# The low part of q in the first block's attention scores: one zero-padded tile per head, so that both score products contract over 128 rows

## The chip, the cores and the metric

The kernel runs on one core of one Trainium2 chip. The metric is the device time of one execution in microseconds (us); less is better. The kernel before takes 2581.49 us (median of 3 runs, 2580.72 to 2582.58).

## The reference

Two transformer blocks of two layers each follow one another on x of 512 tokens by 1024 features. The change touches the two attention layers of the first block. Both have 16 heads of 64 features; the first is causal stick-breaking attention, the second mixes three dilated causal bands. Cut to the scores:

```python
# layer 0 of the first block
z = jnp.einsum('bhqd,bhkd->bhqk', qb, kh).astype(jnp.float32) * scale      # scale = 64 ** -0.5
log_stay = jnp.where(strict, jax.nn.log_sigmoid(-z), 0.0)
log_after = lax.cumsum(log_stay, axis=3, reverse=True) - log_stay
w = jnp.where(strict, jnp.exp(jax.nn.log_sigmoid(z) + log_after), 0.0)
out = jnp.einsum('bhqk,bhkd->bhqd', w, vh)
# layer 1 of the first block: q and k with rotary, three branches of (window, dilation)
z = jnp.einsum('brhnqd,brhnkd->brhnqk', qb, k_band).astype(jnp.float32) * scale
p = jnp.exp(z - max(z)); o = (p @ v) / sum(p)        # branches merged by their softmax denominators
```

The second block (a gated linear recurrence, a sliding-window attention, two convolutional MLPs) is not changed.

## The kernel before

All matrices are kept as sums of two rounded parts, high and low (`whi`/`wlo` of a weight block, `xh`/`xl` of the activations), and a product of two such sums is three TensorE products. Weights come through a ring of three staged blocks: SyncE loads a block (`wst`), in the second layer GpSimd multiplies it by a norm gain (L267), ScalarE makes `whi` (L286), VectorE makes `wlo` (L295).

The stages run one after the other: stick-breaking attention (`stick`), an MLP, dilated attention (`dilated`), an MLP, and then the second block, which holds the sliding-window attention (`window`). In each attention stage the heads are taken in eight pairs p = 0 to 7 of 128 features. `weave` writes two sequences alternately into the one program order of each engine: the large projections ("linear" work, pieces of some 24 products), and the attention steps. A step of `stick` makes the scores of one unit (`s1`: products over 128 rows, a mask product with `causal`, then `Abs`, `Exp`, `Ln` on ScalarE), the softplus and its two parts on VectorE (`s1b`), and the cumulative sums of the unit before (`s2`, products with `ntri` and `nones`). A step of `dilated` transposes the probabilities of the unit two steps back (`d2`, L1165, products with `ident`), makes the scores of a unit (`d1`), takes their maximum (L1144) and exponential, and normalizes the unit one step back (`dn`, L1157).

Within a head the 128 rows of TensorE are used like this. Tile `sk[h]` holds the high part of k in the head's own 64 rows and the low part in the other 64. Tile `sq[h]` holds the high part of q in the own rows and all of q in the others, so one product over 128 rows gives k_high·q_high + k_low·q. The missing k_high·q_low is a second product over the 64 own rows, with tile `ql`, which both heads of the pair share (head 0 has rows 0 to 63, head 1 rows 64 to 127). A unit's scores are therefore products of 128, 64, 128, 64 rows, one after the other, of 128, 256, 384 or 512 columns; such a group of four is called a quad below. There are 4 quads in a pair of heads, 32 in each of the two stages. In `stick` k is the operand that is loaded as weights, in `dilated` q is.

`pair_tiles` gives a pair its tiles: two rotating sets, and for every third pair (p = 2, 5) rows of the output tile `o` that are not yet written. `pair_k` (L487, L488) and `pair_q` (L495 to L497) fill them. The stage `window` of the second block already uses full-height second products: tiles `qp` (and two rows of `o`) whose unused half is set to zero once by GpSimd (L1487), with k and q packed in another way.

Of the kernel before, what the change touches and what calls it, by code (L numbers as in the profile page):

```python
# [8 lines left out]
F32 = mybir.dt.float32  # L9
F32R = mybir.dt.float32r  # L10
# [3 lines left out]
ALU = mybir.AluOpType  # L14
PSUM = bass.MemoryType.PSUM

P = 128
S = 512
# [182 lines left out]
class Ring:  # L201
# [3 lines left out]
    def next(self):  # L205
        self.i += 1
        return self.items[self.i % len(self.items)]


class Prog:  # L210
# [256 lines left out]
        run(side)  # L467


    def pair_tiles(self, pool, o, p):  # L470


        if p % 3 < 2:
            make = lambda n: pool.tile([P, S], F32R, name=n, bufs=2)
        else:
            room = iter([o[i][:, m, :] for m in (7, 6, 5) for i in (0, 1)])
            make = lambda n: next(room)
        t = {n: [make(f"{n}{h}") for h in (0, 1)] for n in ("sk", "sq")}
        t["ql"] = make("ql")
        return t  # L480

    def pair_k(self, t, src, eng=None):

# [7 lines left out]
    def pair_q(self, t, src, dup=None, eng=None):  # L491
        nc = self.nc
        for h in (0, 1):
            own, oth = slice(64 * h, 64 * h + 64), slice(64 - 64 * h, 128 - 64 * h)
            nc.scalar.activation(out=t["sq"][h][own], in_=src[own], func=AF.Copy)  # L495
            (dup or nc.vector).tensor_copy(out=t["sq"][h][oth], in_=src[own])
            self.defer(lambda h=h, own=own: (eng or nc.vector).tensor_tensor(  # L497
                out=t["ql"][own], in0=src[own], in1=t["sq"][h][own].bitcast(F32), op=ALU.subtract))

    def scores(self, out, t, h, lhs, ks, qs, start):  # L500

        own = slice(64 * h, 64 * h + 64)
        a = (t["sk"][h][:, ks], t["sq"][h][:, qs]), (t["sk"][h][own, ks], t["ql"][own, qs])
        for i, (k, q) in enumerate(a):
            self.mm(out, *((k, q) if lhs == "k" else (q, k)), start and i == 0)


# [352 lines left out]
    def stick(self):  # L860
        nc = self.nc
        lin, zr = Ring(self.bank[0:2] + self.bank[7:]), Ring(self.bank[2:6])
        with self.tc.tile_pool(name="stick", bufs=1) as pool:
            o = (pool.tile([P, KT, S], F32R, name="oh"), pool.tile([P, KT, S], F32R, name="ol"))
            identr, ntri = pool.tile([P, P], F32R, name="identr"), pool.tile([P, P], F32R, name="ntri")
            nones, causal = pool.tile([P, P], F32R, name="nones"), pool.tile([P, P], F32R, name="causal")
            consts = []
            for t, n in ((ntri, "ntri"), (causal, "causal")):
                e = pool.tile([P, S], F32, name="e", bufs=2)
# [2 lines left out]
            qk, vs = {}, {}  # L872

            def ev_q(s, c):
                def f(bank):
                    t = self.tmp.tile([P, S], F32, name="sq", bufs=3)
                    nc.vector.scalar_tensor_tensor(out=t, in0=bank, scalar=0.125, in1=self.r_bc, op0=ALU.mult, op1=ALU.mult)
                    qk[2 * s + c] = self.pair_tiles(pool, o, 2 * s + c)
                    self.pair_q(qk[2 * s + c], t)
                return f  # L880

# [171 lines left out]
    def dilated(self):  # L1053
        nc = self.nc
        lin, zr, tr = Ring(self.bank[0:2] + self.bank[7:]), Ring(self.bank[2:4]), Ring(self.bank[4:6])
        nc.scalar.preload_act_table_set("natural_log_exp_and_others")
        with self.tc.tile_pool(name="dil", bufs=1) as pool:
            o = (pool.tile([P, KT, S], F32R, name="oh"), pool.tile([P, KT, S], F32R, name="ol"))
# [2 lines left out]
            lnc = pool.tile([P, S], F32, name="lnc")  # L1061
            for t, n in ((cosr, "cos"), (sinr, "sin"), (lnc, "lncount")):
                self.load_const(t, n)
            qk, vs, st, due = {}, {}, {}, []

            def scaled():
# [12 lines left out]
            def ev_rope(p, part):  # L1079
                def f(bank):  # L1080
                    scale = 0.125 if part else 1.0
                    if not part:
                        qk[p] = self.pair_tiles(pool, o, p)
                    t2 = pool.tile([P, S], F32, name="t2", bufs=2)
                    t3 = pool.tile([P, S], F32, name="t3", bufs=2)
                    d = self.tmp.tile([P, S], F32, name="sq", bufs=3)
                    nc.vector.scalar_tensor_tensor(out=t2, in0=bank, scalar=scale, in1=sinr, op0=ALU.mult, op1=ALU.mult)
                    for a in range(0, P, 32):
                        dst, src = t3[a:a + 32, :], t2[a ^ 32:(a ^ 32) + 32, :]
                        if p:  # L1090
                            nc.sync.dma_start(out=dst, in_=src)
                        elif a < 64:
                            nc.scalar.activation(out=dst, in_=src, func=AF.Copy)
                        else:
                            nc.vector.tensor_copy(out=dst, in_=src)
                    nc.vector.scalar_tensor_tensor(out=d, in0=bank, scalar=scale, in1=cosr, op0=ALU.mult, op1=ALU.mult)
                    add = lambda: (nc.gpsimd if p else nc.vector).tensor_tensor(out=d, in0=d, in1=t3, op=ALU.add)
                    eng = nc.gpsimd if p > 1 else nc.vector
                    parts = lambda: self.pair_q(qk[p], d, eng, nc.gpsimd) if part else self.pair_k(qk[p], d, eng)
                    if p:  # L1100
                        due.append([7 if p == 1 else 3, add])
                        due.append([10 if p == 1 else 5, parts])
                    else:
                        add()
                        due.append([0, parts])
                return f
# [582 lines left out]
```

## Time and profile before

| | |
|---|---|
| median of 3 runs | 2581.49 us |
| the profiled execution | 2584.21 us, of it span 2582.3 us |
| TensorE (PE) busy | 2533.5 us, 98% of the span, 12732 products |
| VectorE (DVE), ScalarE (ACT), GpSimd (POOL) busy | 60%, 40%, 17% |
| stick-breaking attention with its projections | about 30 to 268 us of the span |
| dilated attention with its projections | about 660 to 906 us |
| sliding-window attention of the second block | from about 2037 us |

The busy time of PE is a sum of modelled durations of products that overlap; how fast products follow each other is read from their start times. A row of the timeline gives the start and the duration of an instruction (or, with xN, of several alike), its engine, its line, the tile written and the tiles read, and the shape: `64*128 64x256` is a product over 64 rows with 256 columns.

### The profile page before, as it was taken

What the parts mean: (1) busy time and instruction counts of PE and PEld (TensorE: products, weight loads), DVE (VectorE), ACT (ScalarE), POOL (GpSimd) and SP (SyncE); (2) the same over time, 40 slices, a digit from 0 to 9 for tenths busy, and PEclk for the clock granted to TensorE, in tenths of its full rate; (3) what the DMA queues carried; (4) which work ended last, traced back from release to release, by engine and by line L of the source; (5) the groups of instructions that cost most, each with busy time, mean ns of one, the idle gap of its engine ahead of it and who ended that gap; (6) DMA issues with size and microseconds to landing.
All of it is one profiled execution on the core that took longest, in us unless ns stands there. A gap on an engine that the chain in (4) does not pass through costs nothing.

```text
span 2582.3 us, 32942 instructions
## 1 busy us (share of the span) xinstructions
PE 2533.5 (98%) x12732; PEld 2097.1 (81%) x12732; DVE 1557.3 (60%) x2580; ACT 1045.8 (40%) x1736; POOL 443.6 (17%) x394
## 2 busy tenths in 40 slices
PE   9999999999999999999999999999999999999998
PEld 7777888888767788888888888788888777888887
DVE  7665643444767654444476667764556788745556
ACT  6666422223344442222333333443333574534243
POOL 2112100001545210000111124200102326100103
PEclk9999999999989999999999999899999999999998
DMA  4111222232312122222221112232322312232321
GB/s 146 51 49 48 92 98 98 89 102 96 103 58 77 62 96 92 98 98 99 98 95 58 66 37 78 82 113 92 98 97 83 107 50 74 93 103 88 100 93 55
DMA packets 71277, 220.19 MB, mean 85 GB/s; under 512 B 8741, under 2 KB 15013, under 8 KB 71120
## 3 DMA queue, kind: packets, MB, share of 16 engines
q1 hardware_dynamic: 70512, 216.57, 25.5%
q8 instruction: 100, 1.64, 0.3%
q0 software_dynamic: 464, 1.27, 0.2%
q14 instruction: 57, 0.47, 0.1%
q10 hardware_dynamic: 144, 0.25, 0.0%
HBM read 209.14 MB, written 5.24 MB: 83 GB/s over the span
## 4 chain that ended last, share of the span: by engine, by line
PE 88%; DVE 8%; ACT 2%; issue 1%; DMA 0%; SPq 0%; POOL 0%; DVEq 0%; ACTq 0%
PE bank L225 87%; DVE wlo L295 1%; DVE lt L640 1%; DVE pr L1548 1%; PE bank L1165 1%; ACT whi L286 1%; DVE pr L1157 0%; DVE pr L1535 0%; DVE ln_sm L545 0%; DVE hg L1265 0%; PE bank L1558 0%; DVE hq L1342 0%; DVE xl L653 0%; DMA x<-in_xT 0%; DVE sm L1538 0%
## 5 line engine op out<-in xcount | busy, mean ns | idle before, releaser
L286 ACT ACTIVATE whi<-wst 128x1024 fp32r<-128x1024 f32 (+2 forms) x410 | 411.1, 1008 | 936.5 <-PE bank L225 750.1
L225 PE MATMUL bank<-xh,whi 128*128 128x512 f32 (+1 forms) x1992 | 780.9, 392 | 7.3 <-DVE xh L650 4.8
L225 PE MATMUL bank<-xl,whi 128*128 128x512 f32 (+1 forms) x1992 | 773.5, 388 | 5.0 <-DVE xl L653 2.7
L225 PE MATMUL bank<-xh,wlo 128*128 128x512 f32 (+1 forms) x1992 | 770.5, 387 | 2.3 <-DVE wlo L295 2.3
L295 DVE TENSOR_TENSOR wlo<-wst,whi 128x1024 fp32r<-128x1024 f32 (+2 forms) x392 | 486.4, 1246 | 100.9 <-ACT whi L286 97.4
L225 PEld LDWEIGHTS bank<-xh,whi 128*128 128x128 f32 x1992 | 379.9, 191 | 90.3 <-issue 14.8
L225 PEld LDWEIGHTS bank<-xl,whi 128*128 128x128 f32 x1992 | 379.0, 190 | 85.8 <-DVE xl L653 6.8
L225 PEld LDWEIGHTS bank<-xh,wlo 128*128 128x128 f32 x1992 | 379.9, 191 | 74.4 <-DVE wlo L295 3.7
L225 PE MATMUL bank<-hh,whi 128*128 128x512 f32 (+1 forms) x760 | 285.4, 375 | 0.0
L225 PE MATMUL bank<-hl,whi 128*128 128x512 f32 (+1 forms) x760 | 284.2, 374 | 0.0
L225 PE MATMUL bank<-hh,wlo 128*128 128x512 f32 (+1 forms) x760 | 284.2, 374 | 0.0
L527 POOL TENSOR_TENSOR acc<-acc,sq 128x512 f32<-128x512 f32 x35 | 50.0, 1428 | 789.6 <-ACT sq L526 789.2
L770 DVE TENSOR_TENSOR x<-x,bank 128x512 f32<-128x512 f32 x96 | 65.9, 688 | 187.4 <-PE bank L225 187.4
L225 PEld LDWEIGHTS bank<-hh,wlo 128*128 128x128 f32 x760 | 143.2, 188 | 25.7 <-issue 0.5
L225 PEld LDWEIGHTS bank<-hh,whi 128*128 128x128 f32 x760 | 143.2, 188 | 25.7 <-issue 0.5
L225 PEld LDWEIGHTS bank<-hl,whi 128*128 128x128 f32 x760 | 143.2, 188 | 25.2
L574 POOL TENSOR_TENSOR x<-x,r_bc 128x512 f32<-128x512 f32 x32 | 46.5, 1462 | 480.4 <-ACT r_bc L572 419.9
L225 PE MATMUL bank<-whi,xh 128*128 128x256 f32 x416 | 122.0, 293 | 0.0
L225 PE MATMUL bank<-wlo,xh 128*128 128x256 f32 x416 | 119.5, 287 | 0.0
L225 PE MATMUL bank<-whi,xl 128*128 128x256 f32 x416 | 119.5, 287 | 0.0
L1410 DVE SCALAR_TENSOR_TENSOR b<-bank,vecs,b 128x511 f32<-128x511 f32 x88 | 65.9, 749 | 85.8 <-ACT b L1408 84.2
L1410 DVE SCALAR_TENSOR_TENSOR a<-bank,vecs,a 128x511 f32<-128x511 f32 x88 | 65.9, 749 | 83.8 <-ACT a L1408 82.2
(285 smaller groups left out, 3537.2 us busy)
## 6 DMA issues: line engine op xcount, KB each, us to landing
wst<-in_w SPq DMA_DIRECT2D x314, 512.0 KB, 3.2
wst<-in_w SPq DMA_DIRECT2D x64, 448.0 KB, 3.1
wst<-in_w SPq DMA_DIRECT2D x36, 256.0 KB, 2.7
t<-t SPq DMA_DIRECT2D x56, 64.0 KB, 2.0
rel_scratch<-sq SPq DMA_DIRECT2D x16, 192.0 KB, 2.1
x<-in_xT SPq DMA_DIRECT2D x8, 256.0 KB, 6.2
bias<-rel_scratch SPq DMA_DIRECT2D x16, 128.0 KB, 2.9
out_dram<-x SPq DMA_DIRECT2D x16, 128.0 KB, 1.8
```

The source lines that it names most:

```text
L225: self.nc.tensor.matmul(out, lhsT=l, rhs=r, start=start, stop=True, skip_group_check=True)
L286: self.nc.scalar.activation(out=self.split[i][0][:, 0:n], in_=self.staged[i][:, 0:n], func=AF.Copy)
L295: (eng or self.lo_eng or self.nc.vector).tensor_tensor(out=lo[:, 0:n], in0=st[:, 0:n], in1=hi[:, 0:n].bitcast(F32), op=ALU.subtract)
L527: self.defer(lambda: eng.tensor_tensor(out=self.acc, in0=self.acc, in1=sq, op=ALU.add))
L574: nc.gpsimd.tensor_tensor(out=self.x[:, j, :], in0=self.x[:, j, :], in1=self.r_bc, op=ALU.subtract)
L640: nc.vector.scalar_tensor_tensor(out=t, in0=self.x[:, m, cs], scalar=gm, in1=self.acc[:, cs], op0=ALU.mult, op1=ALU.mult)
L770: self.nc.vector.tensor_tensor(out=self.x[:, m, :], in0=self.x[:, m, :], in1=bank, op=ALU.add)
L1165: nc.tensor.transpose(bk[:, P * j:P * j + P], pr[h][:, P * j:P * j + P], self.ident)
L1410: nc.vector.scalar_tensor_tensor(out=t[:, sh:S], in0=bank[:, 0:S - sh], scalar=self.vec(f"cw{l}{tap}", f), in1=t[:, sh:S], op0=ALU.mult, o ...
L1548: nc.vector.tensor_scalar(out=pr[h][:, 0:W], in0=pr[h][:, 0:W], scalar1=sm[:, 4 + h:5 + h], scalar2=None, op0=ALU.mult)
```

## The change

`pair_tiles`, called once for each pair, is replaced by `pair_sets`, called once at the start of each of the two stages: three fixed sets, used by p % 3, each with a tile `ql` for each head. The half of `ql[h]` that isn't the head's own is set to zero there by GpSimd, six memsets of 64x512 in each stage. `pair_q` writes only the own half. `scores` multiplies all 128 rows of `sk[h]` with all 128 rows of `ql[h]`. Each set now has six tiles where it had five, two tiles more in SBUF for the two sets outside `o`, and the scratch space of the software DMA queue is cut to 4096 bytes per partition.

```diff
-    def pair_tiles(self, pool, o, p):
-        if p % 3 < 2:
-            make = lambda n: pool.tile([P, S], F32R, name=n, bufs=2)
-        else:
+    def pair_sets(self, pool, o):
+        sets = []
+        for n in range(3):
             room = iter([o[i][:, m, :] for m in (7, 6, 5) for i in (0, 1)])
-            make = lambda n: next(room)
-        t = {n: [make(f"{n}{h}") for h in (0, 1)] for n in ("sk", "sq")}
-        t["ql"] = make("ql")
-        return t
+            make = (lambda name: pool.tile([P, S], F32R, name=name)) if n < 2 else (lambda name: next(room))
+            sets.append({t: [make(f"{t}{h}_{n}") for h in (0, 1)] for t in ("sk", "sq", "ql")})
+            for h in (0, 1):
+                self.nc.gpsimd.memset(sets[n]["ql"][h][64 - 64 * h:128 - 64 * h].bitcast(F32), 0.0)
+        return sets
...
             self.defer(lambda h=h, own=own: (eng or nc.vector).tensor_tensor(
-                out=t["ql"][own], in0=src[own], in1=t["sq"][h][own].bitcast(F32), op=ALU.subtract))
+                out=t["ql"][h][own], in0=src[own], in1=t["sq"][h][own].bitcast(F32), op=ALU.subtract))
...
     def scores(self, out, t, h, lhs, ks, qs, start):
-        own = slice(64 * h, 64 * h + 64)
-        a = (t["sk"][h][:, ks], t["sq"][h][:, qs]), (t["sk"][h][own, ks], t["ql"][own, qs])
-        for i, (k, q) in enumerate(a):
+        k = t["sk"][h][:, ks]
+        for i, q in enumerate((t["sq"][h][:, qs], t["ql"][h][:, qs])):
             self.mm(out, *((k, q) if lhs == "k" else (q, k)), start and i == 0)
...
+            sets = self.pair_sets(pool, o)
...
-                    qk[2 * s + c] = self.pair_tiles(pool, o, 2 * s + c)
+                    qk[2 * s + c] = sets[(2 * s + c) % 3]
...
-    nc = bacc.Bacc("TRN2", target_bir_lowering=False, num_devices=1)
+    nc = bacc.Bacc("TRN2", target_bir_lowering=False, num_devices=1, dynamic_dma_scratch_size=4096)
```

On PE, VectorE, ScalarE and SyncE the sequence of instructions is the same before and after but for the names of tiles; on GpSimd twelve memsets come in, at two places. The first is the start of `stick`, between the sums of squares of the first norm (`acc`) and the loads of two constants (`e`, the masks `ntri` and `causal` before rounding); `sp` behind them belongs to the first attention step:

```order
-L527 TENSOR_TENSOR acc<-acc,sq 128x512 x7
+L526 TENSOR_TENSOR acc<-acc,sq 128x512 x7
+L479 MEMSET ql_0_203 64x512
+L479 MEMSET ql_0_204 64x512
+L479 MEMSET ql_1_211 64x512
+L479 MEMSET ql_1_212 64x512
+L479 MEMSET oh 64x512
+L479 MEMSET ol 64x512
 L238 DMA e<-in_consts 128x128 x2
 L950 TENSOR_TENSOR sp<-sp 128x128 x2
```

The two loads are now issued behind six memsets. The second place is the start of `dilated`, between the loads of the rotary tables and of the band table (`cosr`, `sinr`, `lnc`) and the gains of three staged weight blocks (`wst`):

```order
 L238 DMA cosr<-in_consts 128x512
 L238 DMA sinr<-in_consts 128x512
 L238 DMA lnc<-in_consts 128x512
+L479 MEMSET ql_0_4708 64x512
+L479 MEMSET ql_0_4709 64x512
+L479 MEMSET ql_1_4716 64x512
+L479 MEMSET ql_1_4717 64x512
+L479 MEMSET oh 64x512
+L479 MEMSET ol 64x512
 L267 TENSOR_TENSOR wst<-wst,vecs 128x1024 x3
```

Here the gains of three weight blocks stand behind the memsets.

## Rows read from the trace of the kernel before

**Rows 1.** The page: the chain that ended last, shares of the span by engine.

```profile
PE 88%; DVE 8%; ACT 2%; issue 1%; DMA 0%; SPq 0%; POOL 0%; DVEq 0%; ACTq 0%
```

**Rows 2.** Busy time by stretch: stick, start of dilated, rest of dilated; instructions in brackets.

```profile
41.00:262.00 221.00, 220.88 (x1180) 173.71 (x1179) 146.50 (x237) 151.96 (x298) 40.30 (x64) 1.00 0.16 53
686.00:752.00 66.00, 54.58 (x235) 39.19 (x234) 51.65 (x89) 25.38 (x58) 36.29 (x25) 0.87 0.27 80
752.00:904.00 152.00, 151.97 (x837) 117.62 (x838) 104.25 (x264) 73.70 (x177) 60.95 (x45) 1.00 0.22 67
```

**Rows 3.** Timeline of PE in stick: quads of 256, 128 and 512 columns.

```profile
41.16 0.28 PE L225 MATMUL bank<-sq,sk 128*128 128x256 f32 x1
41.37 0.38 PE L225 MATMUL bank<-ql,sk 64*128 64x256 f32 x1
41.68 0.39 PE L225 MATMUL bank<-sq,sk 128*128 128x256 f32 x1
...
42.31 0.33 PE L225 MATMUL bank<-sq,sk 128*128 128x128 f32 x1
...
43.33 0.50 PE L225 MATMUL bank<-causal,identr 128*128 128x256 f32 x2
...
57.74 0.39 PE L225 MATMUL bank<-sq,sk 128*128 128x512 f32 x1
...
59.34 0.44 PE L225 MATMUL bank<-causal,identr 128*128 128x128 f32 x2
```

**Rows 4.** Timeline of PE in window: quads whose four products all have 128 rows.

```profile
2055.42 0.28 PE L225 MATMUL bank<-sk,qp 128*128 128x128 f32 x1
...
2055.76 0.45 PE L225 MATMUL bank<-xh,whi 128*128 128x512 f32 x1
...
2057.20 0.28 PE L225 MATMUL bank<-sk,oh 128*128 128x256 f32 x1
...
2057.67 0.40 PE L225 MATMUL bank<-xh,whi 128*128 128x512 f32 x1
...
2061.06 0.36 PE L225 MATMUL bank<-sk,oh 128*128 128x256 f32 x1
2061.26 0.28 PE L225 MATMUL bank<-sk,qp 128*128 128x256 f32 x1
```

**Rows 5.** Timeline of PE in dilated: first row of and behind quads, 128 and 512 columns.

```profile
779.00 0.30 PE L225 MATMUL bank<-sk,sq 128*128 128x128 f32 x1
...
780.00 0.50 PE L225 MATMUL bank<-xh,whi 128*128 128x512 f32 x1
...
798.93 0.47 PE L225 MATMUL bank<-sk,sq 128*128 128x512 f32 x1
...
800.61 0.39 PE L225 MATMUL bank<-whi,xh 128*128 128x256 f32 x1
```

**Rows 6.** PE's waits, 660 to 906 us: us in total, times, longest.

```profile
PE bank L1165 <- DVE pr L1157: 8.2, 6, 3.6
```

**Rows 7.** Timeline of one dilated step: DVE's first and last work, PE's transposes behind it.

```profile
798.78 0.69 DVE L1087 SCALAR_TENSOR_TENSOR t<-bank,sinr 128x512 f32<-128x512 f32 x1 [1.73 <-PE bank L225]
...
803.85 0.75 DVE L1157 TENSOR_SCALAR pr<-pr,sm 128x384 f32<-128x384 f32 x2
...
805.02 0.82 PE L1165 MATMUL bank<-ident,pr 128*128 128x128 f32 x6
```

**Rows 8.** GpSimd's memsets of 64x512 in window, by tile: ns min/median/max.

```profile
L1487 POOL MEMSET qp<- x6: 518/519/662, 2007.3 to 2009.8; 64x512 f32 x6
```

**Rows 9.** Timeline at the two places of the memsets, and who uses what follows.

```profile
23.77 1.09 POOL L238 DMA_DIRECT2D e<-in_consts  x2
...
41.17 0.22 DVE L903 CAST ntri<-e 128x128 fp32r<-128x128 f32 x1
...
658.88 3.75 POOL L267 TENSOR_TENSOR wst<-wst,vecs 128x1024 f32<-128x1024 f32 x2
...
663.40 2.01 ACT L286 ACTIVATE whi<-wst 128x1024 fp32r<-128x1024 f32 x2 [6.80 <-PE bank L225]
```

More of the change, by code (lines that the diff above doesn't have):

```diff
@@ L1063, in dilated @@
                 self.load_const(t, n)
+            sets = self.pair_sets(pool, o)
             qk, vs, st, due = {}, {}, {}, []
@@ L1082, in f @@
                     if not part:
-                        qk[p] = self.pair_tiles(pool, o, p)
+                        qk[p] = sets[p % 3]
                     t2 = pool.tile([P, S], F32, name="t2", bufs=2)
```

## The prediction

> **What bounds the kernel now.** I read the page first: the chain that ended last is PE for 88% of the span [rows 1], so time that PE saves counts unless something takes its place. Next came the stretches of the two stages that change, since an average over the span says nothing of them [rows 2]. In the stick-breaking stage (41 to 262 us) PE is busy for 220.88 of 221 us, ScalarE for 152 and VectorE for 147: PE alone sets the pace. The dilated stage is two stretches. From 752 to 904 us PE is busy for 151.97 of 152 us, VectorE for 104. [...] Among PE's waits in this stage the longest in sum is that of the transposes for the normalized probabilities `pr`, 8.2 us in six waits, VectorE's work [rows 6]. Last I read single quads in the timeline, by start times.
>
> **What the change removes.** In stick a quad of 256 columns starts at 41.16 and the next at 42.31: 1.15 us for four products [rows 3]. Within it they start 0.31 us apart (41.37, 41.68), whether the step goes from 128 to 64 rows or back. The sliding-window stage makes the same sort of quad, two products into a bank, twice, with own weights for each, but all four over 128 rows: from 2057.20 to 2057.67, 0.12 us each [rows 4]. So a change of height costs some 0.19 us, and a stick quad has four: between its four products and in front of what follows. The clock isn't the reason: it is granted in full in this stretch [rows 2]. [...]
>
> Stick quads now: 128 columns 43.33 - 42.31 = 1.02 us; 256 columns 1.15; 512 columns 59.34 - 57.74 = 1.60; for 384 I take the mean of the last two, 1.38 [rows 3]. Sum 5.15 us for a head pair.
>
> The same quads at full height: 256 columns 0.47 [rows 4]. 128 columns: the last three products of such a quad take 2055.76 - 2055.42 = 0.34, 0.113 each, so 0.45 for four. 512 columns: between 2055.76 and 2057.20 lie six products of 512 columns, 0.24 each, so 0.96. 384 columns: the mean of 0.47 and 0.96, 0.71. Sum 2.59 us. A pair saves 5.15 - 2.59 = 2.56 us, eight pairs **20.5 us**.
>
> Dilated quads now: 1.00 us at 128 columns, 1.68 at 512 [rows 5]; the sizes in between by the mean 1.34, sum 5.36. At full height the first product behind transposes starts its successor after 0.20 us (2061.06 to 2061.26) and not 0.12 [rows 4], so each quad costs 0.08 more than in stick; and the quad that is followed by products with 64 output columns keeps a switch of another kind, for which I take 0.1, an estimate between nothing and the 0.19 of a change of height. Sum 2.59 + 0.32 + 0.10 = 3.01. A pair saves 2.35 us; the six pairs from 752 us on **14.1 us**, the two before it 4.7.
>
> **What of it is lost.** In stick no other engine comes near: with 20 us gone ScalarE is busy for 152 of some 201 us. I take off 1 us for steps at the stage's end where exponentials hand a bank back late, an estimate; bounds 0 and 3. In dilated the margins are narrow. VectorE works without a break from 798.78 to 804.60, from the end of a column of linear work on PE to the last `pr`, and the transposes that need it start at 805.02: 0.42 us of room [rows 7]. The quad between them loses 1.68 - 1.04 = 0.64, so PE then waits 0.2, and 0.3 where the room is less. I allow 0.3 for one step in four of the 24 in this stretch: 1.8 us, bounds 0 and 7 (every step). In the 66 us before, where VectorE sets the pace, what PE saves mostly turns into longer waits for `pr`; the bounds are 0 and 4.7, and I take 2, as PE's quads do stand in the chain in places. [...]
>
> **What the change adds.** Rows of zeros cost PE nothing beyond the full-height pace: the window quads read above have them too, in `qp`. Six memsets of 64x512 are put on GpSimd's queue in each stage; at 0.52 us [rows 8] that is 3.1 us twice. In stick they delay the loads of the mask constants from 23.77 to 26.9; VectorE takes them at 41.17, 14 us later [rows 9], and GpSimd's next work is an attention step's: nothing. In dilated they stand in front of weight gains: two gains take 658.88 to 662.63, so 1.87 each, and would now run from 662.0 to 665.7. ScalarE begins two `whi` at 663.40; the first has its gain from earlier, the second (at about 664.4) needs the first of these two, done at 663.9: 0.5 us of room. If that cover were gone, ScalarE, then `wlo`, then the norm's statistics behind `wlo` on VectorE would be late by the same amount, at worst 1 us. I take 0. The smaller descriptor scratch changes no instruction; I take 0, with 0 and 5 us as bounds (an early load of three that had to wait for another's landing). VectorE's and ScalarE's work is the same in number and size.
>
> **Sum.** 20.5 - 1.0 + 14.1 - 1.8 + 2.0 = 33.8 us. The profiled execution took 2584.21 us, so 2550.4 for one like it; that run lies 2.7 us above the median, and the prediction goes by the median: 2581.49 - 33.8 = **2548 us**, 1.3% less.
>
> **Rivals.**
> - *VectorE takes over in dilated.* If its chain from projection to `pr` is as tight in all steps as at 798.78, PE's saving in this stage turns into waits: 20.5 - 1 = 19.5, so 2562 us. For it: 0.42 us of room [rows 7]. Against it: VectorE has 48 us idle of 152, and one wait per step costs at most 0.3 of 0.6 saved. Chance 0.13.
> - *All of it and the clock.* No step is bound elsewhere and the half-clock stretch goes: 20.5 + 14.1 + 4.7 + 8.6 = 47.9, so 2534 us. For it: denser products. Against it: VectorE's waits remain. Chance 0.08.
> - *The change doesn't do what it says.* The 0.19 us comes from something else in these quads (two products in a row into one bank, new weights each time) and stays: 2581 us, with 1 us for memsets 2582. Against it: the window stage's quads have both and run at 0.12. Chance 0.03.
> - *Slower by the clock.* [...] Chance 0.02.
> - *Slower by lost overlap.* If the half-height products of head 0 (rows 0 to 63) and head 1 (rows 64 to 127) ran beside other products, 64 of the 128 would be free today, and at full height cost 0.12 to 0.24, 0.18 on average: 11.5 us, 2593. [...] It decides where a half-height product now takes less of PE's time than a full one; it takes 0.31 against 0.12 [rows 3, 4], as a full-height product always stands between two of them. Chance 0.01.
>
> **How the numbers follow.** The forecast's own case has 0.73 and spans 2542 to 2554 (loss terms at their bounds in part). To leave out no more than 2 in 10, the range reaches towards the first two rivals: **2539 to 2560 us**. A change within 0.2% (5 us, about what this kernel's measurement can tell from none) comes from the third rival, 0.03; slower by more from the last two, 0.03; faster has 0.94.
>
> **What would show it.** In the changed profile products of `ql` read 128*128, a 256-column quad in stick takes about 0.5 us, and the stretch from the first to the last quad in stick is some 20 us shorter. In dilated from its first full PE stretch on it is 12 to 14 us shorter, with waits of PE for `pr` of a few tenths. Wrong would be: starts still 0.3 us apart; more half clock than 17 us in dilated; `whi` in ScalarE waiting for a gain near 664 us; waits for `pr` in every step.

## The result and the profile after

The changed kernel took **2542.16 us**, the median of 4 runs (2539.21 to 2547.36), beside 2581.1 us before (4 runs, 2579.26 to 2582.58): a ratio of **0.9852, 95% interval 0.9833 to 0.9871**. The forecast was 2548 us in a range of 2539 to 2560. The profiled execution took 2539.21 us, with a span of 2537.4; beside the profiled one of before (2584.21) that is 45.0 us less, so some 6 us of what the two traces show is more than the medians do. Where these 6 us lie matters below.

The page of after, busy time by engine and the shares of the chain that ended last:

```profile
PE 2485.7 (98%) x12732; PEld 2085.5 (82%) x12732; DVE 1558.2 (61%) x2580; ACT 1044.8 (41%) x1736; POOL 452.1 (18%) x406
PE 87%; DVE 8%; ACT 2%; issue 1%; DMA 1%; SPq 0%; POOL 0%; DVEq 0%; ACTq 0%; POOLq 0%
```

PE still is 87% of the chain [rows 1], with the same 12732 products in the same order; the 12 more instructions on GpSimd are the memsets. The stick quads of after, as [rows 3] shows those of before:

```profile
40.79 0.28 PE L225 MATMUL bank<-sq,sk 128*128 128x256 f32 x1
40.91 0.28 PE L225 MATMUL bank<-ql,sk 128*128 128x256 f32 x1
41.03 0.28 PE L225 MATMUL bank<-sq,sk 128*128 128x256 f32 x1
41.15 0.28 PE L225 MATMUL bank<-ql,sk 128*128 128x256 f32 x1
41.27 0.22 PE L225 MATMUL bank<-sq,sk 128*128 128x128 f32 x1
...
55.27 0.39 PE L225 MATMUL bank<-sq,sk 128*128 128x512 f32 x1
55.49 0.39 PE L225 MATMUL bank<-ql,sk 128*128 128x512 f32 x1
...
56.17 0.33 PE L225 MATMUL bank<-causal,identr 128*128 128x128 f32 x2
56.34 0.39 PE L225 MATMUL bank<-sph,ntri 128*128 128x384 f32 x1
```

Products of `ql` now have 128 rows and start 0.12 us behind the one ahead, not 0.31; a quad of 256 columns takes 0.48 us where it took 1.15, one of 512 columns 0.90 where it took 1.60. The stretches that answer to [rows 2], each from the first quad of its stage to just behind the last, with dilated split at the third pair's first quad (length, then PE, PE's loads, DVE, ACT, POOL busy, granted clock, DMA share, GB/s):

```profile
40.79:232.34 191.55, 191.40 (x1149) 164.87 (x1147) 141.93 (x230) 146.22 (x286) 40.44 (x62) 1.00 0.18 59
663.60:721.39 57.79, 45.26 (x238) 35.64 (x237) 49.12 (x89) 25.44 (x58) 36.87 (x25) 0.94 0.30 92
721.39:852.18 130.79, 128.86 (x801) 107.24 (x800) 101.23 (x251) 68.86 (x170) 61.68 (x45) 1.00 0.22 69
```

Between the same instructions of before lie 214.72, 66.32 and 144.24 us, so the stages gave 23.2, 8.5 and 13.4 us, and nothing else in the kernel moved by more than 1.2: from the stick stage to the first dilated quad it takes 431.27 us instead of 430.07, behind dilated 1685.2 instead of 1685.8, and ahead of stick 40.79 instead of 41.16. The six differences add to 44.9, the difference of the two spans. In dilated PE is no longer busy without a break: 1.9 us of 130.79 are idle, where before there was none. Its waits for the normalized probabilities in that stretch (us in sum, times, longest), of after:

```profile
PE bank L1166 <- DVE pr L1158: 1.2, 2, 1.0
PE bank L1166 <- ACT pr L1150: 0.7, 1, 0.7
```

### The profile page after: what moved, and what is told of

Read it like the earlier page. It is cut to its first block, busy times and chain, and to the rows that moved or that the text cites. A ratio compares the mean times of both kernels' runs of the same rounds, so it can differ in the third digit from the quotient of the medians.

```text
span 2537.4 us, 32954 instructions
## 1 busy us (share of the span) xinstructions
PE 2485.7 (98%) x12732; PEld 2085.5 (82%) x12732; DVE 1558.2 (61%) x2580; ACT 1044.8 (41%) x1736; POOL 452.1 (18%) x406
## 4 chain that ended last, share of the span: by engine, by line
PE 87%; DVE 8%; ACT 2%; issue 1%; DMA 1%; SPq 0%; POOL 0%; DVEq 0%; ACTq 0%; POOLq 0%
PE bank L225 86%; DVE wlo L295 1%; DVE lt L639 1%; DVE pr L1549 1%; PE bank L1166 1%; ACT whi L286 1%; DVE pr L1536 0%; DVE ln_sm L544 0%; DVE pr L1158 0%; DVE hg L1266 0%; PE bank L1559 0%; DVE hq L1343 0%; DVE sm L1539 0%; DVE xl L652 0%; DVE pr L1145 0%
## 5 line engine op out<-in xcount | busy, mean ns | idle before, releaser
L225 PEld LDWEIGHTS bank<-xh,whi 128*128 128x128 f32 x1992 | 378.9, 190 | 86.7 <-issue 13.5
```

The costliest lines, as they stand in the source:

```text
L225: self.nc.tensor.matmul(out, lhsT=l, rhs=r, start=start, stop=True, skip_group_check=True)
```

## The experiments

Profiles of one kernel differ by several microseconds in the stretch in which dilated starts, so whole times come from several runs, and the stages from each kernel's own trace. All ratios are to the kernel before on the same chip: 2583.09 us (17 runs) for the first four, 2582.71 us (15 runs) for the next four; the last three are single runs for their profiles.

**Each stage alone.** `e1_stick_only` keeps the old tiles and heights in dilated, `e2_dilated_only` keeps them in stick; the stage that keeps them has no memsets either. Against the changed kernel, the first (the second has the same in the stick stage):

```diff
     def scores(self, out, t, h, lhs, ks, qs, start):
-        k = t["sk"][h][:, ks]
-        for i, q in enumerate((t["sq"][h][:, qs], t["ql"][h][:, qs])):
+        own = slice(64 * h, 64 * h + 64) if "half" in t else slice(0, P)
+        a = (t["sk"][h][:, ks], t["sq"][h][:, qs]), (t["sk"][h][own, ks], t["ql"][h][own, qs])
+        for i, (k, q) in enumerate(a):
...
-                        qk[p] = sets[p % 3]
+                        qk[p] = self.pair_tiles(pool, o, p)
```

> Full-height second products in the stick-breaking stage alone; the dilated stage as before. If each change between 64 and 128 rows costs PE some 0.19 us and nothing else matters, this stage gives the 23 us that the two traces show between its first and last quad (quads 41.2 us before, 20.1 after, and 0.05 us less on each product behind a quad): 2581 - 23 = 2558 us, and the half-clock stretches of the dilated stage stay at about 17 us. If a part of the gain comes from the sets or the scratch and not from the height, it is another number.

> Full-height second products in the dilated stage alone. If the two stages add up, it gives the rest of the 39 us: 2581 - 16 = 2565 us. If the lesser half clock in the dilated stage (17 us of it before, 7 in the profile of the changed kernel) belongs to the change, the profile has about 7 us of it again and the time may be as low as 2560; if it is chance, it may have 17 and the time is up to 2570.

Measured: 2556.16 us (4 runs, 2552.19 to 2557.91), ratio 0.9899 (0.9884 to 0.9913), and 2567.88 us (6 runs, 2566.11 to 2571.52), ratio 0.9948 (0.9936 to 0.9959). The shares, 1.01% and 0.52%, add to 1.53%; both together gave 1.48%. The windows of the first, in the order of those above:

```profile
40.66:232.18 191.52, 191.38 (x1148) 164.94 (x1147) 141.87 (x230) 146.14 (x286) 40.45 (x62) 1.00 0.18 59
662.24:721.47 59.23, 53.13 (x239) 39.87 (x237) 48.38 (x89) 25.65 (x58) 36.24 (x25) 0.88 0.30 89
721.47:865.71 144.24, 144.21 (x802) 111.10 (x800) 99.49 (x253) 69.84 (x170) 60.66 (x45) 1.00 0.21 63
```

and of the second:

```profile
41.02:255.75 214.73, 214.60 (x1149) 168.26 (x1147) 142.69 (x230) 146.15 (x286) 39.44 (x62) 1.00 0.16 52
687.21:751.25 64.04, 47.68 (x238) 37.74 (x237) 52.70 (x89) 25.67 (x58) 36.76 (x25) 0.89 0.27 83
751.25:884.06 132.81, 129.28 (x801) 107.22 (x800) 103.09 (x251) 68.86 (x170) 61.31 (x45) 1.00 0.23 68
```

The first and third line of each show a stage that depends on its own quads alone: 191.5 us with full height and 214.7 without, 132.8 with and 144.2 without. The middle line goes against the quads: it is short (59.2) where dilated is unchanged and long (64.0) where it is changed. What shortens this stretch is something else.

**All but the height.** `e3_all_but_height` is the changed kernel, with its sets, memsets and smaller scratch, but the second product of a score again takes its head's 64 rows alone:

```diff
-        k = t["sk"][h][:, ks]
-        for i, q in enumerate((t["sq"][h][:, qs], t["ql"][h][:, qs])):
+        own = slice(64 * h, 64 * h + 64)
+        a = (t["sk"][h][:, ks], t["sq"][h][:, qs]), (t["sk"][h][own, ks], t["ql"][h][own, qs])
+        for i, (k, q) in enumerate(a):
```

> All of the change (fixed sets, a ql tile for each head, twelve memsets, the smaller scratch), but the second product again over the head's own 64 rows. If the height alone makes the gain, the time is that of the kernel before and the memsets' price, 2581 to 2583 us, with quads as long as before (1.15 us at 256 columns). If the sets or the placement in memory make part of it, it lies under 2575.

Measured: 2583.09 us (12 runs, 2577.02 to 2585.38), ratio 0.9999 (0.999 to 1.0009). Its PE timeline is that of before [rows 3], 0.3 us apart:

```profile
41.02 0.28 PE L225 MATMUL bank<-sq,sk 128*128 128x256 f32 x1
41.23 0.38 PE L225 MATMUL bank<-ql,sk 64*128 64x256 f32 x1
41.53 0.39 PE L225 MATMUL bank<-sq,sk 128*128 128x256 f32 x1
...
42.16 0.33 PE L225 MATMUL bank<-sq,sk 128*128 128x128 f32 x1
```

So the whole gain is the height of the second product; the tiles, the memsets and the scratch together give and cost nothing that the whole time can tell.

**The half-height products side by side.** `e4_halves_together` is the kernel before with the order within a quad changed: both heads' first products, then both heads' second products. Each quad then has two changes of height in place of four, and the two half-height products, on rows 0 to 63 and 64 to 127 and into different banks, are neighbours:

```diff
-                    for h in (0, 1):
-                        self.scores(banks[h][:, o0:o0 + S - P * j], qk[p], h, "k", slice(P * j, P * j + P), slice(P * j, S), n == 0)
+                    for part, h in ((0, 0), (0, 1), (1, 0), (1, 1)):
+                        self.scores(banks[h][:, o0:o0 + S - P * j], qk[p], h, "k", slice(P * j, P * j + P), slice(P * j, S), n == 0, part)
...
-                for h in (0, 1):
-                    self.scores(banks[h][:, 0:W], qk[p], h, "q", slice(0, W), slice(P * i, P * i + P), True)
+                for part, h in ((0, 0), (0, 1), (1, 0), (1, 1)):
+                    self.scores(banks[h][:, 0:W], qk[p], h, "q", slice(0, W), slice(P * i, P * i + P), True, part)
```

> The kernel before, with the four products of a quad in another order: the two of 128 rows, then the two of 64 rows (the same work, the same tiles). If the cost is one of changing the height, a quad has two changes where it had four, a 256-column quad takes about 1.15 - 0.38 = 0.77 us, and the 64 quads give up to 24 us, less the dilated stage's waits: about 2561 us. If it is a cost of each half-height product, whatever stands beside it, quads stay at 1.15 us and the time at 2581. If half-height products on different rows also run beside each other, the two start a few ns apart and a 256-column quad takes about 0.65 us: 2556.

Measured: 2554.3 us (4 runs, 2551.72 to 2556.51), ratio 0.9893 (0.9879 to 0.9908). Its PE timeline, a stick quad of 512 columns (the view puts products alike into one row; x2 is two):

```profile
56.01 0.62 PE L225 MATMUL bank<-sq,sk 128*128 128x512 f32 x2
56.55 0.50 PE L225 MATMUL bank<-ql,sk 64*128 64x512 f32 x2
56.98 0.44 PE L225 MATMUL bank<-causal,identr 128*128 128x128 f32 x2
```

The two products of `ql` stand in one row of 0.50 us, where a single one of them has 0.497 us in the kernel before (the mean of twelve), so by an estimate from these two figures they start some 8 ns apart at most; and the two together pass in the 0.43 us that a single one took before. Even so the quad takes 0.97 us where full height takes 0.90: one product of 0.23 us is hidden, but the two changes of height cost more than that, 0.97 - 3 x 0.227 = 0.29 us (0.227 us is the mean of three steps at full height, 55.27 to 55.95 in after). Stick takes 198.55 us in this order, 214.72 before and 191.55 after.

**The memsets.** `a1_changed_again` is the changed kernel once more, `e5_memsets_on_vector` has the dilated stage's six memsets on VectorE:

```diff
-                self.nc.gpsimd.memset(sets[n]["ql"][h][64 - 64 * h:128 - 64 * h].bitcast(F32), 0.0)
+                eng.memset(sets[n]["ql"][h][64 - 64 * h:128 - 64 * h].bitcast(F32), 0.0)
...
-            sets = self.pair_sets(pool, o)
+            sets = self.pair_sets(pool, o, nc.vector)
```

> The changed kernel once more, unchanged, for a second profile. If the lesser half clock at the start of the dilated stage (7 us against 17) belongs to the changed kernel, it is there again and the two profiles agree in that stretch within 1 us. If it is chance of the execution, the half clock lies anywhere from 7 to 17 us and the stretch differs by up to 5 us, while the stick stage and the rest of the dilated stage agree within 0.3 us.

> The changed kernel with the six memsets of the dilated stage on VectorE, which is idle there for 8 us, and not on GpSimd. If the memsets push the weight gains on GpSimd so that these run beside wlo on VectorE and slow it (two wlo took 3.67 us, 2.36 before), PE's wait for dg falls from 1.3 us to some 0.6 and the first quad of the dilated stage comes 1.2 us earlier against the last of stick; the whole time is 1 us less, within the spread of runs. If the memsets cost nothing, nothing moves.

Measured: 2541.94 us (4 runs, 2538.88 to 2545.65), ratio 0.9841 (0.9825 to 0.9856), and 2542.44 us (5 runs, 2538.59 to 2545.49), ratio 0.9842 (0.9827 to 0.9856): not to be told apart by the whole time, where 1 us less was expected of the second. By the stage they are: from stick to the first dilated quad the memsets on VectorE give 429.96 us, those on GpSimd 431.3, the kernel before 430.1. The timeline of after, at the place of [rows 9]:

```profile
635.23 2.19 POOL L479 MEMSET ql<- 64x512 f32 x4
637.46 0.52 POOL L479 MEMSET oh<- 64x512 f32 x1
638.04 0.52 POOL L479 MEMSET ol<- 64x512 f32 x1
638.53 3.73 POOL L267 TENSOR_TENSOR wst<-wst,vecs 128x1024 f32<-128x1024 f32 x2
639.73 2.01 ACT L286 ACTIVATE whi<-wst 128x1024 fp32r<-128x1024 f32 x2 [6.80 <-PE bank L225]
640.83 3.67 DVE L295 TENSOR_TENSOR wlo<-wst,whi 128x1024 fp32r<-128x1024 f32 x2 [8.37 <-ACT whi L286]
644.41 0.15 DVE L552 TENSOR_SCALAR small<-bank 128x4 f32<-128x4 f32 x1
```

and of the kernel with the memsets on VectorE:

```profile
632.37 2.37 DVE L479 MEMSET ql<- 64x512 f32 x4 [0.17 <-issue]
...
640.57 2.36 DVE L295 TENSOR_TENSOR wlo<-wst,whi 128x1024 fp32r<-128x1024 f32 x2 [4.57 <-ACT whi L286]
642.85 0.15 DVE L552 TENSOR_SCALAR small<-bank 128x4 f32<-128x4 f32 x1
```

ScalarE's `whi` doesn't wait: 2.01 us for the two, as before. But GpSimd's gains, 3.3 us later than they would be, now run from 638.53 to 642.26, and the second of them beside the first of VectorE's two `wlo`: this one takes 2.53 us instead of 1.23, the other 1.21 as ever, so the two take 3.67 us instead of 2.36. The norm's statistics behind them are 1.3 us late, and PE waits for what is made of them (tile `dg`) for 1.6 us instead of 0.6. The second gain and the first `wlo` of after by themselves, and the same `wlo` with the memsets on VectorE:

```profile
640.38 1.88 POOL L267 TENSOR_TENSOR wst<-wst,vecs 128x1024 f32<-128x1024 f32 x1
640.83 2.53 DVE L295 TENSOR_TENSOR wlo<-wst,whi 128x1024 fp32r<-128x1024 f32 x1 [8.37 <-ACT whi L286]
...
640.57 1.23 DVE L295 TENSOR_TENSOR wlo<-wst,whi 128x1024 fp32r<-128x1024 f32 x1 [4.57 <-ACT whi L286]
```

If `wlo` stands still until the second gain ends, the two end at 642.26 + 2.36 = 644.62; they end at 644.50, and in `e3`, which has the same memsets, the same sum gives 668.17 where 668.03 is measured. So in both traces the first `wlo` is late as if it stood still until the gain ends, to 0.14 us; what holds it isn't shown.

**The clock where dilated starts.** What the middle stretch shows is part chance. One more profile of after and two more of before were taken for it:

> The kernel before, unchanged, profiled again. If where the half clock falls at the start of the dilated stage is chance, the 66 us from that stage's first quad to the second quad of p = 2 take another time here, by 2 to 8 us, with the same instructions; if the first profile is typical, 66 us within 1 us and half clock of about 17 us.

> As the run before it: a third profile of the kernel before, for the same stretch; chance gives three values spread over several us, a typical first profile three equal ones.

> A third profile of the changed kernel. The stretch took 57.8 us in the first and 60.5 in the second; if the change itself shortens it by 2 us and the rest is chance, the three lie about 2 us under the three of the kernel before on average, with overlapping spreads; if it shortens it by 6 us or more, all three lie under all three of before.

Measured: 2576.36 and 2583.14 us before, 2545.86 after (one run each). Windows of that stretch, from the first dilated quad to the third pair's: of the kernel before,

```profile
685.95:752.27 66.32, 54.90 (x239) 39.51 (x237) 51.70 (x89) 25.65 (x58) 36.61 (x25) 0.87 0.27 80
```

of its second profile,

```profile
686.13:745.58 59.45, 52.71 (x239) 39.10 (x237) 48.53 (x89) 25.37 (x58) 36.54 (x25) 0.89 0.29 89
```

and of its third,

```profile
687.12:751.09 63.97, 54.59 (x239) 39.57 (x237) 50.12 (x89) 25.64 (x58) 36.62 (x25) 0.87 0.27 83
```

then of `a1_changed_again`,

```profile
663.43:723.93 60.50, 46.96 (x238) 37.90 (x237) 51.29 (x89) 25.43 (x58) 36.93 (x25) 0.92 0.29 88
```

and of `a2_changed_third`:

```profile
663.65:728.11 64.46, 47.62 (x239) 37.14 (x237) 53.06 (x89) 25.55 (x58) 36.80 (x25) 0.89 0.27 82
```

Before: 66.3, 59.5, 64.0, mean 63.2. After: 57.8, 60.5, 64.5, mean 60.9. The granted clock is 0.87 to 0.94 in the mean. In the two profiles first compared it is either 1.00 or 0.50 in this stretch, and 0.50 in pieces: before from 690.6 to 694.0, 711.1 to 721.3 and 738.4 to 741.8 us, after from 679.5 to 682.9 and 706.8 to 710.2. At 0.50, half clock, the means stand for 7 to 17 us (0.87 over 66.32 us is 2 x 0.13 x 66.32 = 17): in the order of the profiles 17, 14 and 17 us before, 7, 10 and 14 after. Within either kernel the shortest stretch is the one with the least half clock; across the two this doesn't hold, since 14 us go with 59.5 before and with 64.5 after. The kernel's own gain of 2.3 us in the means is smaller than the spread of either kernel; three profiles each don't settle it. What all three show is a turn of work into waits: PE is busy for 54.1 us of the stretch in the mean before and for 46.6 after, and idle for 9.2 and 14.3.

The rest of dilated wasn't as steady as `a1_changed_again` expected: behind this stretch the changed kernel takes 130.8, 132.8 and 130.7 us in its three profiles, not the same within 0.3; before it was 144.2 each time.

To see what the half clock costs, `e6_fill_before` is the kernel before with ten more products in front of the second and the fourth step of dilated, into a bank that nobody reads, and `e7_fill_after` the same in `e5_memsets_on_vector`. They add work and take none away:

```diff
+                    for _ in range(10 if t in (1, 3) else 0):
+                        self.mm(self.bank[6], self.xn[0][:, 0, 0:P], self.xn[0][:, 0, :], True)
```

> The kernel before with 20 more products of 512 columns, whose result nobody reads (10 each ahead of two steps at the start of the dilated stage, in an idle bank, where PE waits for VectorE). They cost 4.6 us of PE at full clock. If the half-clock stretches there (17 us in the profile) cost what they seem to (up to 8.6 us) and come from PE's waits, they shrink and the time falls to 2575-2580 us or stays; if VectorE alone sets the pace there and the clock costs nothing, the time is that of before or up to 4.6 us more.

> The changed kernel with the memsets of the dilated stage on VectorE and the same 20 unread products. If the clock is what spreads its runs (2539 to 2547 us), half clock in that stretch is gone, the runs lie closer together and at 2537 to 2541 us; if not, the time is 2542 us or up to 4.6 us more.

Measured: 2578.6 us (11 runs, 2576.32 to 2581.74), ratio 0.9983 (0.9974 to 0.9992), and 2539.84 us (4 runs, 2538.1 to 2541.69), ratio 0.9832 (0.9818 to 0.9845). The stretches of [rows 2], 686 to 752 and 752 to 904 us, in `e6`:

```profile
686.00:752.00 66.00, 57.15 (x274) 41.69 (x274) 52.95 (x97) 26.63 (x63) 36.42 (x25) 0.95 0.27 80
752.00:904.00 152.00, 151.39 (x828) 116.27 (x827) 105.41 (x260) 72.93 (x173) 60.60 (x44) 1.00 0.22 67
```

With twenty products that nobody needs the old kernel is 4.1 us faster (2582.71 - 2578.6), and its runs spread over 5.4 us instead of 8.5. The clock there is 0.95 in this profile, where the three of before have 0.87 and 0.89. That it is the clock that gives the time is supported by the whole runs, for which the mean granted clock is on record: 0.987 to 0.990 in the eleven with the extra products (mean 0.9892) and 0.985 to 0.988 in the fifteen without (0.9866), that is some 56 and 69 us of half clock in an execution, if all that is missing is at 0.50; and the fastest of the fifteen, 2578.54 us, has 0.988, the slowest, 2587.04, has 0.985. By the stage it isn't shown: from the first dilated quad to the end of dilated this profile takes 208.8 us, the three of before 210.6, 203.7 and 208.2. In the changed kernel the same products leave 0.91 in the stretch, so half clock isn't gone from it as the expectation had it, and the 2.6 us by which it is below its twin lie within the intervals of both. So it is the fastest median of the study by a margin that isn't established.

The same record of whole runs speaks for the change itself raising the clock. On the chip of the last experiments the changed kernel has a mean of 0.9885 (`a1`, 4 runs) and 0.9878 (`e5`, 5 runs) against 0.9866; on the chip of the first ones `e2`, with dilated at full height, has 0.9880 (6 runs), while `e1` and `e3`, with dilated as it was, have 0.9872 (4 and 12 runs) beside 0.9871 before (17 runs). That is 5 to 11 us less of half clock in an execution, counted the same way, and it goes with full height in dilated.

## Why the prediction was right

The mechanism is what the prediction took it for, and its time lies 6 us from the median, within the range. By its own terms:

- **Stick, 20.5 less 1.0 forecast, 23.2 measured.** The size was off, on two counts. The quads themselves gave 21.0 us (all 32 took 41.17 us before and 20.13 after, from first start to the start of what follows): at 512 columns a full-height quad takes 0.90 us and not the 0.96 read from rows 4. The products behind a quad gained too, which wasn't counted: the two mask products at 56.17 hand over after 0.17 us where those at 59.34 [rows 3] took 0.27 before (the next product starts at 59.61), over the stage 2.1 us. And the loss at the stage's end didn't come: PE is busy for 191.40 of 191.55 us.
- **Dilated from the third pair on, 14.1 less 1.8 forecast, 11.4 to 13.5 measured** (144.24 against 132.81 in `e2`, 132.77 in `a1`, 130.79 in after, 130.72 in `a2`). Both parts hold: the quads add up to 5.37 us before and 2.92 after for a pair, 14.7 for six; the last product of a quad that is followed by products with 64 output columns hands over after 0.26 to 0.27 us in after, where those ahead of it take 0.17 to 0.18, so the 0.1 taken for that switch is there; and PE waits for `pr` for 1.9 us, in three waits and not in every step, though up to 1.0 us long where a few tenths were forecast. In `a1` the waits for VectorE's `pr` alone are 3.4 in four.
- **The two pairs before it, 2 forecast.** The means differ by 2.3, under a spread of 5 to 7 in either kernel: neither shown nor refuted in size. That most of PE's saving turns into waits there is what the profiles show. The 8.5 us of the two traces first compared are for the most part chance of the execution. The forecast's sum has no term for the clock; by the whole runs some 5 to 11 us of half clock go, worth at most half of that, and what part of it the 2.3 us hold isn't separated.
- **Memsets, 0 forecast, 1.2 us lost.** The step that failed is what a late gain does: the prediction looked for a gain that comes late for `whi` in ScalarE and found 0.5 us of room; 0.3 us was left (the gain ends at 640.42, `whi` starts at 640.70), so `whi` didn't wait. It missed that a gain, once late, runs beside `wlo`. The bound, "at worst 1 us", was a little too low, for another reason than its own. Scratch: nothing, as forecast.

In the mean of the three profiles of each kernel the stages gave 23.7 (stick; one profile of before has a piece of half clock there and takes 216.3 us, without it 23.2), 12.8 and 2.3 (dilated), -1.2 (memsets) and 0.4 us (all the rest): 38.0 us. The medians differ by 38.9 us, with 33.3 to 43.1 by the interval, and by 40.8 in the second comparison (37.2 to 45.2). The stages' sum lies in both. Of the 5 us by which the forecast of 33.8 fell short, stick's 3.7 are the greater part. That the 2 us of the first two pairs meet the difference of the means, 2.3, is luck, with spreads of 5 us and more.

**The rivals.** *VectorE takes over in dilated* would have left 144 us there; `e2` has 132.8. *All of it and the clock*, 2534 us, is below every run: 14.7 us less waits is what the quads gave, and of the half clock a part went, not all. Its 8.6 us are what a granted clock of 0.87 takes from 66 us [rows 2], and no run shows that term: the three profiles of after have 0.94, 0.92 and 0.89 there. *The change doesn't do what it says* falls with `e3`. *Slower by the clock*: the rest of dilated is granted 1.00 as before. *Slower by lost overlap* fails where the prediction said, at the full-height product between two half-height ones, which start 0.31 us apart [rows 3]; `e4` shows that the overlap is real once they are neighbours, two in 0.43 us, so the rival was right on the chip and wrong on the order of this kernel.

One reading was coarser than the rows. Starts 0.31 us apart "whether the step goes from 128 to 64 rows or back" holds inside a quad, but the first step into half height costs less: 41.16 to 41.37 is 0.21 us against 0.12 at full height, and every later change 0.31 [rows 3]. A quad so pays 0.09 + 3 x 0.19 = 0.66 us; at 256 columns 1.15 became 0.48. The forecast summed whole quads and was not touched by it.

## What to carry

Where products of different height alternated on PE here, each change cost time (0.09 to 0.2 us) that a look at busy shares didn't show: compare the starts of such products with those of the same size elsewhere in the kernel, and price the edit from that; padding to one height with zeros was better here than setting the half-height products side by side (0.90 and 0.97 us for a quad of 512 columns). An engine that gets new work ahead of its old doesn't only make that work late, it moves it beside other work, as the gain here beside a `wlo` that then took 2.53 us and not 1.23: look at what will run next to it, and not only at who waits for it. And where a stretch has half clock that differs between executions, as here from 7 to 17 us, take several profiles of both kernels before giving its difference to the edit.

## What the runs showed of the hardware

- Two half-height products on different rows and banks, one behind the other in `e4`, together take the 0.43 us that one took between full-height ones; at 512 columns the quad is 0.97 us, at full height 0.90.
- A gain of 128x1024 on GpSimd ran when VectorE started a `wlo` of the same size, and that `wlo` took 2.53 us, 1.23 with the memsets on VectorE.
- Twenty unneeded products took the mean granted clock of the runs of before from 0.9866 to 0.9892 and their median from 2582.71 to 2578.6 us: here added work of PE cost less than it gave back.
- The amount of half clock differs between executions of one kernel: 14 to 17 us before and 7 to 14 after, at the start of dilated in three profiles each.
